# State-space loop: additions and tables moved to GpSimd, coefficients and scan in PSUM, input products in three passes

## The chip, the cores and the metric

The kernel runs on one core of a Trainium2 chip. Five engines of that core work at once, each through its own instructions in a fixed order: TensorE (PE; its weight loads are shown apart as PEld), VectorE (DVE), ScalarE (ACT), GpSimd (POOL) and SyncE (SP), which issues most DMA transfers. A wait at the head of an engine's order holds everything behind it. The metric is the device time of one execution, in microseconds (us). A profiled execution also has a span, from its first instruction to its last.

## The reference

Two residual layers over a sequence of 512 tokens and 1024 channels, all in float32. Layer 0 mixes tokens with a grouped state-space layer (S5), layer 1 with forgetting attention; each is followed by a gated feed-forward part. The change concerns the state-space layer alone:

```python
u = h @ w_in                                  # 512 x 1024, weights 1024 x 1024
lb = exp(lre*dt) * (cos(lim*dt), sin(lim*dt)) # 64 groups of 64 complex states
bb = k * b                                    # complex coefficients, 16 channels a group
state[t] = lb * state[t-1] + bb @ u[t]        # within each group
y[t] = Re(c @ state[t]) + d_skip * u[t]
y = gelu(y); y = y * sigmoid(y @ w_glu); out = y @ w_out
```

Here `h` is the normed input, scaled and shifted by columns that are computed from a conditioning vector.

## The kernel before

Channels lie on the 128 partitions: 8 channel tiles (`KT`) of 128 channels, each with 8 groups, that is 4 pairs of groups. Tokens are cut into 64 blocks of 8 (`L` = 8, `B` = 64). A state is carried from block to block; inside a block a small kernel of matrix products does the work.

The start of the S5 stage is under a manual schedule for PE, ACT, DVE and SP: there these engines take the instructions in the order in which the code is written. GpSimd, and everything behind that part, is put in order by the scheduler. In the start the scale and shift columns are made (`ada_pe`, matrix products over weights that stream in), the scaled input `a_x` is made by 8 DVE instructions, the input product of tile 0 is taken from it without its shift (the shift is added by `u_shift` afterwards), and `s5_params` makes on the DVE, with many small instructions, the powers and coefficients of the states: `s_pr`, `s_pi` (called `er`, `ei` as views), `s_lr`, `s_li`, and `s_mag`. Then the shift is added to `a_x` on the ACT, and `s5_tables` makes the first three doublings of the rotation table `s_rot`.

The loop runs over tiles m = 0 to 7. For each tile:

- `inputs(m)`: 8 products in float32 (weights `raw`, input `a_x`) give the input projection in a PSUM bank of pool `mm`; ACT copies it out (`uf`); it goes through DRAM to the layout `u`.
- `s5_inputs(m)`: `s5_outer` makes the coefficients `x` on the DVE, two multiplications of 1024 elements per partition and an addition. `x` has one buffer, its partner `x2` two. PE multiplies them by `s_cd` (line 993) and transposes them (line 1004); ACT copies `ktt`, `kt` and `w1` out; `kt` goes through DRAM (`s_z`) and comes back as `tw`, from which ACT makes `t`.
- `s5_scan(m)`: PE makes products of `w1` and `u` in a PSUM bank of pool `aux` (line 1026); the DVE turns them with `s_rot`, scans them along the blocks with the factors `cf`, and turns them back to the states `ua`.
- `s5_states_out(m)`: `s5_outer` again, from `er`, `ei` and `cc`, gives `w2`.
- `s5_outputs(m)`: PE products of `t` and `u` (line 1068) and of `w2` and `ua` (line 1076), then the gelu on the ACT.
- every second tile `s5_tables` doubles the table three times for the next 8 pairs (9 instructions).

Both PSUM pools, `mm` and `aux`, have 4 banks. `raw()` takes a weight buffer by its third argument from one of three rings: `raw` (3 buffers), `w_hi` (5) or `w_lo` (5, through `rest`). Elsewhere in the kernel float32 products are made in three passes (`mms`): operand and weight are each split into a part rounded to float32r (hi) and a rest (lo), and hi by hi, hi by lo and lo by hi are summed.

## Time and profile before

| what | value |
|---|---|
| time, median of 3 runs | 1182.35 us (1181.65 to 1184.41) |
| the profiled execution | 1181.21 us |
| its span | 1179.1 us |
| PE clock granted, mean | 0.997 |
| busy: PE, DVE, ACT, POOL | 1161.2, 970.3, 642.4, 99.1 us |

In the rows of a group, "out<-in" gives the tiles by name, then shapes as partitions x elements, then the count, the busy time and the mean of one in ns. A timeline row gives the start, the time from the first start to the last end of the instructions in it, the engine, the line, and in brackets the idle time ahead of it with what ended it. Two instructions of one engine overlap a little: a DVE instruction of 1.22 us starts 1.14 us after one of its kind. A row of the chain gives start, length, engine, tile and line. One float32 matrix product shows as two PE records of 128x512. Line numbers are those of the kernel before; behind the change they are a few higher.

### The profile page before, as it was taken

What the parts mean: (1) busy time and instruction counts of PE and PEld (TensorE: products, weight loads), DVE (VectorE), ACT (ScalarE), POOL (GpSimd) and SP (SyncE); (2) the same over time, 40 slices, a digit from 0 to 9 for tenths busy, and PEclk for the clock granted to TensorE, in tenths of its full rate; (3) what the DMA queues carried; (4) which work ended last, traced back from release to release, by engine and by line L of the source; (5) the groups of instructions that cost most, each with busy time, mean ns of one, the idle gap of its engine ahead of it and who ended that gap; (6) DMA issues with size and microseconds to landing.
All of it is one profiled execution on the core that took longest, in us unless ns stands there. A gap on an engine that the chain in (4) does not pass through costs nothing.

```text
span 1179.1 us, 21197 instructions
## 1 busy us (share of the span) xinstructions
PE 1161.2 (98%) x8199; PEld 1015.6 (86%) x8199; DVE 970.3 (82%) x1805; ACT 642.4 (54%) x1150; POOL 99.1 (8%) x157
## 2 busy tenths in 40 slices
PE   7999999999999999999999999999999999999997
PEld 2466688899999999998998788878999989999987
DVE  8899987889878889876675788866999888888855
ACT  2554536346667667665443657644556545555543
POOL 1000000000011111110000534320000000000000
PEclk9999999999999999999999999999999999999998
DMA  9788868815789899887524555423123323333331
GB/s 356 242 259 256 253 199 308 283 54 145 188 248 255 217 252 253 229 240 209 145 89 151 179 193 187 154 72 109 54 84 114 120 89 104 114 113 108 92 88 72
DMA packets 79427, 202.70 MB, mean 172 GB/s; under 512 B 23919, under 2 KB 26191, under 8 KB 78303
## 3 DMA queue, kind: packets, MB, share of 16 engines
q1 hardware_dynamic: 72847, 181.96, 46.5%
q0 software_dynamic: 6192, 18.88, 9.2%
q8 instruction: 64, 1.05, 0.4%
q10 hardware_dynamic: 288, 0.52, 0.1%
q14 instruction: 36, 0.29, 0.1%
HBM read 194.41 MB, written 6.92 MB: 171 GB/s over the span
## 4 chain that ended last, share of the span: by engine, by line
PE 93%; DMA 3%; DVE 2%; ACT 1%; issue 1%; POOL 0%; SPq 0%; DVEq 0%; ACTq 0%; POOLq 0%
PE mmp L308 43%; PE mmp L568 19%; PE aux L568 7%; PE mmp L1186 4%; PE mmp L1366 3%; PE mmp L1216 2%; PE aux L1512 2%; PE aux L1495 2%; PE aux L1076 1%; PE aux L1068 1%; PE mmp L221 1%; PE aux L1465 1%; DMA raw<-in_ada_w 1%; PE aux L1026 1%; DMA nf<-nfd 1%; PE mmp L1153 1%
## 5 line engine op out<-in xcount | busy, mean ns | idle before, releaser
L287 ACT ACTIVATE w_hi<-raw 128x1024 fp32r<-128x1024 f32 (+4 forms) x197 | 173.4, 888 | 125.8 <-PE mmp L308 64.9
L292 DVE TENSOR_TENSOR w_lo<-raw,w_hi 128x1024 fp32r<-128x1024 f32 (+4 forms) x154 | 155.7, 1013 | 30.2 <-ACT w_hi L287 26.4
L308 PE MATMUL mmp<-ghi,w_hi 128*128 128x512 f32 (+1 forms) x392 | 144.1, 368 | 0.0
L308 PE MATMUL mmp<-glo,w_hi 128*128 128x512 f32 (+1 forms) x392 | 143.7, 367 | 0.0
L308 PE MATMUL mmp<-ghi,w_lo 128*128 128x512 f32 (+1 forms) x392 | 143.6, 366 | 0.0
L308 PE MATMUL mmp<-a_hi,w_hi 128*128 128x256 f32 (+1 forms) x440 | 141.0, 323 | 0.0
L308 PE MATMUL mmp<-a_hi,w_lo 128*128 128x256 f32 (+1 forms) x440 | 139.0, 317 | 0.0
L308 PE MATMUL mmp<-a_lo,w_hi 128*128 128x256 f32 (+1 forms) x440 | 138.8, 316 | 0.0
L568 PE MATMUL mmp<-w_hi 128*128 128x256 f32 x420 | 116.3, 277 | 1.2 <-ACT nm_h L575 1.2
L568 PE MATMUL mmp<-w_lo,w_hi 128*128 128x256 f32 x420 | 116.0, 276 | 0.0
L568 PE MATMUL mmp<-w_hi,w_lo 128*128 128x256 f32 x420 | 116.0, 276 | 0.0
L287 ACT ACTIVATE w_hi<-sums 128x1024 fp32r<-128x1024 f32 x78 | 81.8, 1058 | 43.2 <-DVE sums L539 24.2
L292 DVE TENSOR_TENSOR w_lo<-sums,w_hi 128x1024 fp32r<-128x1024 f32 x78 | 94.3, 1218 | 4.0 <-ACT w_hi L287 2.8
L308 PEld LDWEIGHTS mmp<-a_hi,w_hi 128*128 128x128 f32 x440 | 82.2, 188 | 7.1 <-issue 2.6
L308 PEld LDWEIGHTS mmp<-a_hi,w_lo 128*128 128x128 f32 x440 | 82.6, 188 | 6.4
L308 PEld LDWEIGHTS mmp<-a_lo,w_hi 128*128 128x128 f32 x440 | 82.7, 188 | 4.6
L256 DVE CUSTOM_DVE_ANT_0 ada_raw<-ada_raw,ada_c,rest 128x1024 f32<-128x1024 f32 x64 | 83.7, 1324 | 2.3 <-DMA ada_raw<-in_ada_rows 2.2
L308 PEld LDWEIGHTS mmp<-ghi,w_lo 128*128 128x128 f32 x392 | 73.6, 188 | 12.3
L308 PEld LDWEIGHTS mmp<-glo,w_hi 128*128 128x128 f32 x392 | 73.6, 188 | 11.1
L308 PEld LDWEIGHTS mmp<-ghi,w_hi 128*128 128x128 f32 x392 | 73.6, 188 | 11.1
L568 PEld LDWEIGHTS mmp<-w_hi 128*128 128x128 f32 x420 | 78.8, 188 | 1.8 <-ACT nm_h L575 1.8
L568 PEld LDWEIGHTS mmp<-w_lo,w_hi 128*128 128x128 f32 x420 | 78.9, 188 | 0.0
(331 smaller groups left out, 3047.1 us busy)
## 6 DMA issues: line engine op xcount, KB each, us to landing
raw<-in_w_up SPq DMA_DIRECT2D x88, 512.0 KB, 3.4
ada_raw<-in_ada_rows SPq DMA_DIRECT2D x64, 512.0 KB, 4.6
raw<-in_ada_w SPq DMA_DIRECT2D x32, 512.0 KB, 7.0
...
```

The source lines that it names most:

```text
L221: self.last_mm = nc.tensor.matmul(ps[32 * qq:32 * qq + 32, :], self.sc32[:, k, :], w[:, q * S:(q + 1) * S], start=(step is steps[0]), stop ...
L256: nc.vector.tensor_tensor_reduce(w, w, self.crow, 1.0, self.ada_b[:, i, m:m + 1], ALU.mult, ALU.add, self.par[i][:, m:m + 1])
L287: nc.scalar.activation(hi, src, AF.Copy)
L292: self.late = (nc.vector.tensor_tensor(lo, src, hi.bitcast(F32), ALU.subtract).ins,)
L308: self.last_mm = self.nc.tensor.matmul(o, wt, xt[:, cols], start=(k == 0 and n == 0), stop=(k == nk - 1 and n == 2),)
L568: self.last_mm = nc.tensor.matmul(o, wt[:, k], xt[:, k], start=(first and k == 0 and n == 0), stop=(k == H - 1 and n == 2), skip_group_che ...
L1026: nc.tensor.matmul(ps[g2 * 64:(g2 + 1) * 64, ri, k, :], w1[:, k, ri, g2 * 64:(g2 + 1) * 64], u[:, g2 * H4 + k, :], start=(k == 0 and ri == ...
L1186: nc.tensor.matmul(ps, w[m][:, k, :], x[:, k], start=(k == 0), stop=(k == KT - 1))
L1216: nc.tensor.matmul(gps[m], wt, xt[:, k], start=(k == 0 and part == 0 and xt is yhi), stop=(k == KT - 1 and part == 1))
L1366: self.last_mm = nc.tensor.matmul(ps[q, b][:, :n], xt[:, k, tb], wt, start=(k == 0 and i == 0), stop=(k == KT - 1 and i == 2),)
L1495: nc.tensor.transpose(pt[:, r - rs[0], k, :], s[:, r, k * P:(k + 1) * P], self.ident)
L1512: nc.tensor.matmul(pv[:, c * P:], self.v[:, hp, k, r].rearrange("p t d -> p (t d)"), pp[:, r, c + 3 * k:NB + 3 * k, :].rearrange("p b t -> ...
```

## The change

- `parted(m)` splits the input weights of tiles 1 to 7: ACT makes `w_hi`, GpSimd the rest `w_lo`. `part_x(k)` splits the input: ACT adds the shift and rounds (`a_xhi`, in the room that held `h`), DVE makes the rest (`x_lo`). The input products of tiles 1 to 7 are made by `mms`, three float32r passes each in place of one float32 product.
- the 8 `x_lo` take two buffers of the ring `w_hi` and two of `w_lo` through the loop (`self.rooms` = 3 is the number of `w_lo` buffers left); `load_w` uses the ring `raw` alone, and `ada_pe` the rings `raw` and `w_hi`.
- `in_banks` has ACT copy `lr`, `li` into one PSUM bank of `mm` and `er`, `ei` into another; `s5_outer` reads them there (the output coefficients of tile 7 are still made from SBUF).
- the additions of `s5_outer` go from the DVE to GpSimd, and so do the tables for tiles 2, 4 and 6.
- `s5_scan` works in place: the turned values, the scan and the turning back stay in the PSUM bank of the products, which is free when `ua` is written and no longer after the second multiplication.

```diff
     def s5_outer(self, outs, ls, planes, qs, first):
...
-        return nc.vector.tensor_tensor(outs[0], outs[0], outs[1], ALU.add).ins
+        nc.gpsimd.tensor_tensor(outs[0], outs[0], outs[1], ALU.add)
+        return last.ins
...
-        self.x_made = self.s5_outer((x, x2), (self.lr, self.li), self.bb, qs, (1, 0))
+        self.x_made = self.s5_outer((x, x2), self.lp, self.bb, qs, (1, 0))
...
-        m1 = pool.tile([P, 2, W], F32, name="m1")
         m2 = pool.tile([P, 2, W], F32, name="m2")
-        nc.vector.tensor_tensor(m1, v, cb, ALU.mult)
         nc.vector.tensor_tensor(m2, v, sb, ALU.mult)
-        nc.vector.tensor_tensor(m1[:, 0], m1[:, 0], m2[:, 1], ALU.add)
-        nc.vector.tensor_tensor(m1[:, 1], m1[:, 1], m2[:, 0], ALU.subtract)
+        nc.vector.tensor_tensor(v, v, cb, ALU.mult)
+        nc.vector.tensor_tensor(v[:, 0], v[:, 0], m2[:, 1], ALU.add)
+        nc.vector.tensor_tensor(v[:, 1], v[:, 1], m2[:, 0], ALU.subtract)
...
+        line = ps.rearrange("p r g b -> p (r g b)")
+        nc.vector.tensor_tensor_scan(line, cf.rearrange("p r g b -> p (r g b)"), line, 0.0, op0=ALU.mult, op1=ALU.add)
         a = pool.tile([P, 2, H4, B], F32, name="ua", bufs=2)
+        b = pool.tile([P, 2, W], F32, name="ub")
+        nc.vector.tensor_tensor(b[:, 0], v[:, 0], sb[:, 0], ALU.mult)
+        nc.vector.scalar_tensor_tensor(b[:, 1], v[:, 1], -1.0, sb[:, 1], op0=ALU.mult, op1=ALU.mult)
+        nc.vector.tensor_tensor(v, v, cb, ALU.mult)
+        self.scanned = nc.vector.tensor_tensor(a.rearrange("p r g b -> p r (g b)"), v, b[:, ::-1], ALU.add).ins
...
+                def parted(m):
+                    hi = self.wpool.tile([P, KT, P], F32R, name="w_hi", bufs=WB)
+                    nc.scalar.activation(hi, w[m], AF.Copy)
+                    lo = self.rest([P, KT, P])
+                    nc.gpsimd.tensor_tensor(lo, w[m], hi.bitcast(F32), ALU.subtract)
+                    w[m] = [(hi[:, k], lo[:, k]) for k in range(KT)]
...
+                    def part_x(k):
+                        b = self.par[i][:, k:k + 1]
+                        nc.scalar.activation(xhi[:, k], x[:, k], AF.Identity, bias=b)
+                        return nc.vector.scalar_tensor_tensor(
+                            xlo[k], x[:, k], b, xhi[:, k].bitcast(F32), op0=ALU.add, op1=ALU.subtract
+                        )
...
                     for k in range(2):
-                        nc.scalar.activation(x[:, k], x[:, k], AF.Identity, bias=self.par[i][:, k:k + 1])
+                        part_x(k)
+                    parted(1)
...
                     for k in range(2, KT):
-                        nc.scalar.activation(x[:, k], x[:, k], AF.Identity, bias=self.par[i][:, k:k + 1])
-                    behind = [self.s5_signs_c(), next(params), self.s5_tables(slice(0, G // 2), 0, 3), last_mm.ins]
+                        part_x(k)
+                    behind = [self.s5_signs_c(), next(params), self.s5_tables(slice(0, G // 2), 0, 3, nc.vector), last_mm.ins]
...
                     for k in range(m == 1, KT):
-                        nc.tensor.matmul(ps, w[m][:, k, :], x[:, k], start=(k == 0), stop=(k == KT - 1))
+                        self.mms(ps, w[m], split_x, k, KT, slice(0, S))
...
+            self.lp = in_banks(self.lr, self.li)
             with self.behind(*behind):
                 for m in range(2):
                     inputs(m)
                 ws[0] = self.s5_inputs(0)
+            self.ep = in_banks(self.er, self.ei)
...
-                        self.s5_tables(slice(m * 4, m * 4 + 8), 3, 6)
+                        self.s5_tables(slice(m * 4, m * 4 + 8), 3, 6, nc.gpsimd if m else nc.vector)
```

The first place is the DVE in the start of the stage, behind the 8 instructions that make `a_x`. Before, the small instructions of `s5_params` (`s_pr`, `s_pi`, `s_lr` and so on) stand next:

```order
L174 SCALAR_TENSOR_TENSOR ga_100<-aux,rest 128x8
L1137 SCALAR_TENSOR_TENSOR a_x<-h,ga_100,aux 128x512 x8
L892 TENSOR_TENSOR s_w_360<-s_pr 128x128
L893 TENSOR_TENSOR s_w_361<-s_pi 128x128
L894 TENSOR_TENSOR s_pr<-s_w_360,s_w_361 128x4x32
```

After, on the same engine:

```order
L175 SCALAR_TENSOR_TENSOR ga_100<-aux,rest 128x8
L1141 SCALAR_TENSOR_TENSOR a_x<-h,ga_100,aux 128x512 x8
L1174 SCALAR_TENSOR_TENSOR x_lo<-a_x,par_96,a_xhi 128x512 x8
L893 TENSOR_TENSOR s_w_360<-s_pr 128x128
L894 TENSOR_TENSOR s_w_361<-s_pi 128x128
L895 TENSOR_TENSOR s_pr<-s_w_360,s_w_361 128x4x32
```

The eight `x_lo`, which read the shift columns `par_96` and the `a_xhi` of the ACT, stand ahead of the rest of `s5_params`.

The second place is the ACT, from the copy that writes the shift columns (`par_96`) on. Before:

```order
L177 ACTIVATE par_96<-aux 128x8
L1160 ACTIVATE a_x<-a_x,par_96 128x512 x2
L1170 ACTIVATE u_shift<-aux 128x1
L1172 ACTIVATE uf<-mmp,u_shift 128x512
L241 ACTIVATE c_rows<-aux 8x128
L1175 ACTIVATE a_x<-a_x,par_96 128x512 x6
```

After (the four copies `mmp<-...` are those of `in_banks`; the second `w_hi` is that of tile 2):

```order
L178 ACTIVATE par_96<-aux 128x8
L1173 ACTIVATE a_xhi<-a_x,par_96 128x512 x2
L1107 ACTIVATE w_hi<-raw 128x1024
L1191 ACTIVATE u_shift<-aux 128x1
L1193 ACTIVATE uf<-mmp,u_shift 128x512
L242 ACTIVATE c_rows<-aux 8x128
L1173 ACTIVATE a_xhi<-a_x,par_96 128x512 x6
L822 ACTIVATE s_cc<-s_c 128x32x16
L823 ACTIVATE s_cc<-s_c 128x32x32
L826 ACTIVATE s_cd_133<-s_cc 64x64x16 x2
L1210 ACTIVATE uf<-mmp 128x512
L1245 ACTIVATE mmp<-s_lr 128x256
```

A `w_hi` stands ahead of `u_shift`, and with it ahead of six of the eight `a_xhi`; `w_hi` of tile 2 comes behind the copies of `s_lr` and `s_pr`.

The third place is GpSimd in the loop. Before, it has nothing there, only the memsets of the start and the next stage's first:

```order
L833 MEMSET s_cd_133 128x2048
L837 MEMSET s_mask 128x64
L871 MEMSET s_pr 128x32
L872 MEMSET s_pi 128x32
L838 MEMSET s_mask 128x1
L136 MEMSET z_gap 128x32
```

After, the stretch behind the addition of `x` for tile 2, up to that for tile 3 (`x_974`; `w_926` is `w2` of tile 1):

```order
L945 TENSOR_TENSOR s_tab<-s_rot,s_turn 128x128
L946 TENSOR_TENSOR s_tab<-s_rot,s_turn 128x128
L947 TENSOR_TENSOR s_rot<-s_tab 128x2x8x8
L945 TENSOR_TENSOR s_tab<-s_rot,s_turn 128x256
L946 TENSOR_TENSOR s_tab<-s_rot,s_turn 128x256
L947 TENSOR_TENSOR s_rot<-s_tab 128x2x8x16
L960 TENSOR_TENSOR w_926<-w_926,x_927 128x1024
L945 TENSOR_TENSOR s_tab<-s_rot,s_turn 128x512
L946 TENSOR_TENSOR s_tab<-s_rot,s_turn 128x512
L947 TENSOR_TENSOR s_rot<-s_tab 128x2x8x32
L1109 TENSOR_TENSOR w_lo<-raw,w_hi 128x1024
L960 TENSOR_TENSOR x<-x,x_974 128x1024
```

Nine table instructions, the rest of a weight tile and the addition for `w2` stand between two additions of `x`.

More of the change, by code (lines that the diff above doesn't have):

```diff
@@ L85, in __init__ @@
         self.pending = None
+        self.rooms = WB
         self.rests, self.odd, self.by_dma = 0, False, False
@@ L216, in ada_pe @@
             for j, (t, k) in enumerate(step):
-                w = self.raw([P, D], self.io["ada_w"][i, k * P:(k + 1) * P, t * D:(t + 1) * D], n % 3)
+                w = self.raw([P, D], self.io["ada_w"][i, k * P:(k + 1) * P, t * D:(t + 1) * D], n % (3 if self.rooms == WB else 2))
                 n += 1
@@ L943, in s5_tables @@
             im = self.turn[:, k, 1:3, pairs, None].to_broadcast(sh)
-            nc.vector.tensor_tensor(v1, T[:, :, :, :n], re, ALU.mult)
-            nc.vector.tensor_tensor(v2, T[:, ::-1, :, :n], im, ALU.mult)
-            last = nc.vector.tensor_tensor(T[:, :, :, n:2 * n], v1, v2, ALU.add)
+            e.tensor_tensor(v1, T[:, :, :, :n], re, ALU.mult)
+            e.tensor_tensor(v2, T[:, ::-1, :, :n], im, ALU.mult)
+            last = e.tensor_tensor(T[:, :, :, n:2 * n], v1, v2, ALU.add)
         return last.ins
@@ L954, in s5_outer @@
             a = first[n]
-            nc.vector.tensor_tensor(
+            last = nc.vector.tensor_tensor(
                 o.rearrange("p k r c j -> p k (r c) j"), l[:, qs, None, :].to_broadcast(sh),
@@ L958, in s5_outer @@
             )
-        return nc.vector.tensor_tensor(outs[0], outs[0], outs[1], ALU.add).ins
+        nc.gpsimd.tensor_tensor(outs[0], outs[0], outs[1], ALU.add)
+        return last.ins
     def s5_states_out(self, m):
         t1, t2 = (self.s5q.tile([P, GM // 2, 2, CG, L], F32, name=n, bufs=2) for n in ("w2", "x2"))
-        self.s5_outer((t1, t2), (self.er, self.ei), self.cc, slice(m * (GM // 2), (m + 1) * (GM // 2)), (0, 1))
+        self.s5_outer((t1, t2), (self.er, self.ei) if m == KT - 1 else self.ep, self.cc, slice(m * (GM // 2), (m + 1) * (GM // 2)), (0, 1))
         return t1
@@ L1046, in s5_scan @@
             )
-        sg = m2
-        nc.vector.tensor_tensor_scan(
-            sg.rearrange("p r w -> p (r w)"), cf.rearrange("p r g b -> p (r g b)"),
-            m1.rearrange("p r w -> p (r w)"), 0.0, op0=ALU.mult, op1=ALU.add,
-        )
-        a = pool.tile([P, 2, H4, B], F32, name="ua", bufs=2)
-        b = pool.tile([P, 2, H4, B], F32, name="ub", tag="m1")
-        fl = lambda t: t.rearrange("p r g b -> p r (g b)")
-        nc.vector.tensor_tensor(fl(a), sg, cb, ALU.mult)
-        nc.vector.tensor_tensor(fl(b)[:, 0], sg[:, 0], sb[:, 0], ALU.mult)
-        nc.vector.scalar_tensor_tensor(fl(b)[:, 1], sg[:, 1], -1.0, sb[:, 1], op0=ALU.mult, op1=ALU.mult)
-        self.scanned = nc.vector.tensor_tensor(a, a, b[:, ::-1], ALU.add).ins
+        line = ps.rearrange("p r g b -> p (r g b)")
+        nc.vector.tensor_tensor_scan(line, cf.rearrange("p r g b -> p (r g b)"), line, 0.0, op0=ALU.mult, op1=ALU.add)
+        a = pool.tile([P, 2, H4, B], F32, name="ua", bufs=2)
+        b = pool.tile([P, 2, W], F32, name="ub")
[3 more added lines that the diff above has]
+        self.scanned = nc.vector.tensor_tensor(a.rearrange("p r g b -> p r (g b)"), v, b[:, ::-1], ALU.add).ins
         return a
@@ L1105, in load_w @@
                 def load_w(m):
-                    w[m] = self.raw([P, KT, P], self.io["s5_w_in"][m], m % 3)
+                    w[m] = self.raw([P, KT, P], self.io["s5_w_in"][m])
+                def parted(m):
[4 more added lines that the diff above has]
+                    w[m] = [(hi[:, k], lo[:, k]) for k in range(KT)]
                 self.rot = keep.tile([P, 2, G // 2, B], F32, name="s5_rot")
@@ L1158, in s5 @@
                     )
+                    xhi = self.normed("a_hi", WHOLE, "a_xhi")
+                    self.rooms = WB - 2
+                    xlo = []
+                    for n in range(KT // 2):
+                        tag = ("w_hi", f"w_lo{self.rooms + n // 2}")[n % 2]
+                        xlo.append(self.wpool.tile([P, 2 * S + 32 * (n % 2)], F32R, name="x_lo", tag=tag, bufs=(WB, 1)[n % 2]))
+                    xlo = [t[:, S * k:S * k + S] for t in xlo for k in range(2)]
+                    def part_x(k):
[4 more added lines that the diff above has]
+                        )
+                    split_x = lambda k: (xhi[:, k], xlo[k])
                     for k in range(2):
-                        nc.scalar.activation(x[:, k], x[:, k], AF.Identity, bias=self.par[i][:, k:k + 1])
+                        part_x(k)
+                    parted(1)
                     col = self.aux.tile([P, 1], F32, name="aux")
@@ L1164, in s5 @@
                         if k == KT // 2:
-                            nc.tensor.matmul(second, w[1][:, 0, :], x[:, 0], start=True, stop=False)
+                            self.mms(second, w[1], split_x, 0, KT, slice(0, S))
                         last_mm = nc.tensor.matmul(
@@ L1218, in glu_head, with in_banks @@
                         )
+            def in_banks(*ts):
+                o = self.mm.tile([P, S], F32, name="mmp").rearrange("p (n q j) -> p n q j", n=2, j=L)
+                for n, t in enumerate(ts):
+                    nc.scalar.activation(o[:, n], t, AF.Copy)
+                return o[:, 0], o[:, 1]
+            self.lp = in_banks(self.lr, self.li)
             with self.behind(*behind):
```

6 lines of the change are left out of this document (4 added, 2 removed).

## The prediction

> **What bounds the kernel now.** I read the page first (busy time by engine, then the chain that ended last), then the busy time by stretch, then the chain in order of time through the S5 stage.
>
> ```profile
> PE 1161.2 (98%) x8199; PEld 1015.6 (86%) x8199; DVE 970.3 (82%) x1805; ACT 642.4 (54%) x1150; POOL 99.1 (8%) x157
> PE 93%; DMA 3%; DVE 2%; ACT 1%; issue 1%; POOL 0%; SPq 0%; DVEq 0%; ACTq 0%; POOLq 0%
> 37.00:60.34 23.34, 22.59 (x121) 11.15 (x120) 20.26 (x28) 16.23 (x36) 0.00 (x0) 1.00 0.65 201
> 60.34:135.13 74.79, 74.79 (x660) 46.51 (x656) 71.58 (x105) 36.44 (x104) 0.00 (x0) 1.00 0.82 255
> 135.13:178.40 43.27, 43.27 (x388) 35.64 (x385) 36.47 (x55) 19.43 (x48) 0.46 (x5) 1.00 0.70 222
> ```
>
> The last three rows are the run-up to the loop, five periods of it and its tail, with PE, PEld, DVE, ACT, POOL, granted clock, DMA share and GB/s. TensorE bounds everything: 93% of the chain, and no gap at all in the loop and the tail. VectorE comes close there (71.58 of 74.79), GpSimd does nothing. What the change does to the time is therefore two things: PE work that it removes, and PE idle time that it creates. The chain gives both ends of the loop and the unit prices:
>
> ```profile
> 37.93 0.79 PE aux L1166 x8
> 39.68 0.80 PE aux L1166 x8
> ...
> 53.42 0.57 PE aux L993 x16
> 53.99 1.02 PE aux L1004 x8
> 55.02 0.11 PE aux L970
> ...
> 60.41 1.08 PE aux L1026 x32
> 61.50 1.05 PE mmp L1186 x2
> ...
> 82.25 5.15 PE mmp L1186 x12
> ...
> 135.20 1.08 PE aux L1026 x32
> ...
> 178.40 4.99 PE aux L308 x22
> ```
>
> The scan products (L1026) of tile 0 start at 60.41, those of tile 5 at 135.20: 14.96 us a tile. Six float32 products take 5.15, so 0.858 each; 22 float32r passes take 4.99, so 0.227 each and 0.680 for three.
>
> **The change, part by part: the gain.** Tiles 1 to 7 have 56 products (one is L1165). 56 x (0.858 - 0.680) = 10.0 us of PE work go, all on the path. The loop's work falls by 8 x 0.178 to 13.5 a tile. The additions and tables taken off VectorE (two a tile, and nine a pair of tiles) gain nothing of themselves: the chain has 2% DVE.
>
> **The loss: the start.** Here the order decides. VectorE and ScalarE before:
>
> ```profile
> 24.60 5.36 DVE L1137 SCALAR_TENSOR_TENSOR a_x<-h,ga,aux 128x512 f32<-128x512 f32 x8
> 29.87 0.38 DVE L892 TENSOR_TENSOR s_w<-s_pr 128x128 f32<-128x128 f32 x1
> 33.40 0.63 DVE L894 TENSOR_TENSOR s_lr<-s_w,s_w 128x256 f32<-128x256 f32 x1
> 39.02 1.22 DVE L955 TENSOR_TENSOR x<-s_lr,s_bb 128x1024 f32<-128x1024 f32 x1
> 40.16 1.22 DVE L955 TENSOR_TENSOR x<-s_li,s_bb 128x1024 f32<-128x1024 f32 x1
> 41.30 0.28 DVE L944 TENSOR_TENSOR s_tab<-s_rot,s_turn 128x128 f32<-128x128 f32 x1
> ...
> 37.21 1.33 ACT L1160 ACTIVATE a_x<-a_x,par 128x512 f32<-128x512 f32 x2
> 40.51 0.17 ACT L1170 ACTIVATE u_shift<-aux 128x1 f32<-128x1 f32 x1 [1.96 <-PE aux L1166]
> 41.45 3.77 ACT L1175 ACTIVATE a_x<-a_x,par 128x512 f32<-128x512 f32 x6
> 122.37 1.04 ACT L1240 ACTIVATE w_hi<-raw 128x1024 fp32r<-128x1024 f32 x1
> ```
>
> From 29.87 to 39.02 VectorE does 9.15 us of coefficients and tables while it waits for no shift. After, the eight `x_lo` stand ahead of them, and `x_lo` needs the shift. That cover is gone. GpSimd's prices come from the attention stage, the only rows with its elementwise work:
>
> ```profile
> L1443 POOL TENSOR_TENSOR nf<-nf,rest x16: 1284/1296/2257, 647.4 to 771.9; 128x512 f32<-128x512 f32 x16
> L1486 POOL TENSOR_SCALAR s<-s,sm 128x512 f32<-128x512 f32 x16 | 11.9, 754 | 1.1 <-DVE sm L1484 0.8
> L1486 POOL TENSOR_SCALAR s<-s,sm 128x128 f32<-128x128 f32 x16 | 5.7, 371 | 58.8 <-DVE sm L1484 51.1 <-DVE mn L1477 7.6
> 647.45 3.75 POOL L1443 TENSOR_TENSOR nf<-nf,rest 128x512 f32<-128x512 f32 x2 [21.22 <-DMA nf<-nfd]
> 679.66 2.55 POOL L1443 TENSOR_TENSOR nf<-nf,rest 128x512 f32<-128x512 f32 x2 [3.03 <-DMA nf<-nfd]
> ...
> 648.35 1.71 DVE L256 CUSTOM_DVE_ANT_0 ada_raw<-ada_raw,ada_c,rest 128x1024 f32<-128x1024 f32 x1
> 665.68 1.27 DVE L256 CUSTOM_DVE_ANT_0 ada_raw<-ada_raw,ada_c,rest 128x1024 f32<-128x1024 f32 x1
> 679.70 2.20 DVE L292 TENSOR_TENSOR plo<-aux,phi 128x384 fp32r<-128x384 f32 x4
> ```
>
> No row has 1024 elements. The two `TENSOR_SCALAR` rows give a fixed part of about 0.24 us (754 - 371 over 384 elements, carried back to zero); with it the 1.284 of 512 elements makes 2.04 ns an element, so I take 2.33 for 1024, 0.76 for 256, 0.50 for 128. The ends are VectorE's 1.22 and twice the row, 2.57. [...]
>
> The last rows show that the two engines disturb each other. Beside `plo<-aux,phi`, where VectorE reads one operand in PSUM, a GpSimd pair takes 2.55. Beside L256, which reads SBUF twice, it takes 3.75, 1.2 more, and L256 itself 1.71 for 1.27. So 1.7 us of such VectorE work cost GpSimd 1.2. In the loop nearly all VectorE work now has an operand in PSUM; in the start the table instructions do not.
>
> The walk, each step from the rows above:
>
> 1. `a_xhi` 0 and 1 are ready at 38.54, `w_hi` of tile 1 at 39.6 (+1.04), `w_lo` at 41.9 (+2.33). PE, which reaches the third pass of tile 1's first product before the last four shift columns, ends those (+0.23, +0.80) at 42.9; before at 40.48.
> 2. `u_shift`, `uf` and the six other inputs took from 40.51 to 45.22, 4.7 us: now to 47.6. The last `x_lo` (0.67, as one of the eight of `a_x`, 5.36 / 8) ends at 48.3.
> 3. The 9.15 us of coefficients and tables now run from 48.3 to 57.45. `s_lr` is there 4.2 us into them (33.40 + 0.63 before), so ScalarE's four copies (under 0.67 each, the `a_x` pair of twice their size taking 1.33) and tile 2's `w_hi` are ready inside this time.
> 4. Two multiplications (39.02 to 41.30 before) end at 59.75. The addition on GpSimd: 2.33, plus a disturbance, because eight table instructions start on VectorE at the same moment. By the rows below they have 3 x 0.283 + 3 x 0.418 + 2 x 0.686 = 3.5 us; at 1.2 for 1.7 this is up to 2.5, I take 2.0. `x` of tile 0 is there at 64.1.
> 5. PE: L993 and L1004 (0.57, 1.02), 65.7. `x` has one buffer, so VectorE starts tile 1's only now: 1.14 + 0.6 (a table instruction between) + 1.14, 68.6; addition 2.33, 70.9; L993, L1004, L970 (1.7), 72.6. Only then, in PE's order, come the scan products of tile 0: 72.6 for 60.41, 12.2 us late.
>
> ```profile
> L944 DVE TENSOR_TENSOR s_tab<-s_rot,s_turn 128x512 f32<-128x512 f32 x3 | 2.1, 686 | 0.0
> L944 DVE TENSOR_TENSOR s_tab<-s_rot,s_turn 128x256 f32<-128x256 f32 x3 | 1.3, 418 | 0.0
> L944 DVE TENSOR_TENSOR s_tab<-s_rot,s_turn 128x128 f32<-128x128 f32 x3 | 0.8, 283 | 0.0
> L1037 DVE TENSOR_TENSOR m<-aux,s_rot 128x512 f32<-128x512 f32 x5 | 3.4, 684 | 0.5 <-PE aux L1026 0.5
> L1055 DVE TENSOR_TENSOR ua<-m,s_rot 128x512 f32<-128x512 f32 x5 | 3.4, 682 | 0.0
> ...
> 56.33 0.42 SPq L192 DMA_DIRECT2D raw<-in_s_w_in  x1
> ```
>
> By then PE has done 16 products before, 16 2/3 after, with all else equal; the 2/3 is worth 0.45. PE meanwhile has nothing to do: its order holds only tiles 1 and 2, and tile 2 waits for a `w_hi` that stands behind `s_lr`.
>
> **The loop.** With an operand in PSUM (L1037) VectorE takes 684 ns, without (L1055) 682. [...] ScalarE gets 7 x 1.04 and four small copies; it is half idle. Input weights now come from three `raw` buffers and are held until GpSimd has made the rest; behind such a load `u`, `tw` and `s_z` would wait in SP's order. I take nothing: SP issued tile 3's load at 56.33, 5 us before its first product (61.50), and if that cover goes, a load is late by one GpSimd instruction, 0 to 2.6 us.
>
> GpSimd has, for two tiles, 6 x 2.33 and 3 x (0.50 + 0.76 + 1.28): 21.6 us of 27.0. But between the additions of `x` for tiles 2 and 3 stand twelve instructions: 7.6 + 3 x 2.33 = 14.6, more than PE's 13.5. So PE waits about 1 us for each of tiles 3, 5 and 7. The scan's bank of `aux`, held some 8 us longer, and `t` of tile 0, whose way through DRAM begins late, add a little. I take 3 us in all; the ends are 0 (additions of 1.22) and 17 (2.57, and 1.28 for each table instruction: 19.3, 5.8 too many, three times).
>
> **Sum.** + 12.2 (start) - 0.45 - 39 1/3 x 0.178 = 7.0 (products still to come) + 3 (loop) = +7.7. The tail, from 135 to 178, is continuous PE work before, and that work is unchanged. The profiled execution took 1181.21, 1.1 below the median of 1182.35; on the median's scale +7.7 gives 1190.
>
> **Rivals.**
>
> *GpSimd keeps up* (the other side). If its additions take VectorE's 1.22 and nothing disturbs them, the start is 3 x 1.1 + 2.0 shorter, 6.9 late, and the loop waits for nothing: 6.9 - 0.45 - 7.0 = -0.5, 1182. It turns into a gain where float32r passes also suffer less from being interleaved: a lone float32 product costs 1.05 (row at 61.50) for 0.858; three such places a tile at 0.15 less, over five tiles, make -2.3 more, 1179.5. It decides at additions of about 1.3 us. Against it: no GpSimd row is that fast.
>
> *GpSimd bounds the loop.* Table instructions have broadcast and reversed operands of four dimensions, which no row shows on GpSimd. At 2.57 and 1.28 the pair of tiles has 6 x 2.57 + 9 x 1.28 = 26.9 us, all of PE's 27.0, and the waits go towards the 17: 1195 to 1202. For it: the stretch of twelve instructions. Against it: the first rows of GpSimd, undisturbed, are at 1.284 all.
>
> *PSUM banks.* `aux` has four; two hold outputs, one the scan, and with it held through the turning back, L1004 and L970 share one and wait for ScalarE's copies each time. About 1 us a tile: 1196 to 1199.
>
> **How the numbers follow.** This measurement can tell about 0.2% from no change: 1180.0 to 1184.7 is the same. Forecast (1186 to 1194): 0.50. GpSimd bounds: 0.17. Banks: 0.08. GpSimd keeps up: 0.25, of which 0.12 within the same and 0.13 faster. So faster 0.13, same 0.12, slower 0.75. The range, 1180 to 1200, leaves out the gain and the far end of GpSimd's case; by itself the forecast has 1186 to 1194, from the disturbance (0 to 2.5) and the loop (1 to 6).
>
> **What would show it.** Right: VectorE idle from about 29.9 to 38 and again between the first two and the last six `x_lo`; the first `x` multiplication near 57; PE idle for about 14 us between 37 and 72; scan products of tile 0 near 72; then 13.5 to 14.5 us a tile; three passes of a product near 0.68. Wrong: scan products of tile 0 before 67, or a loop period above 15 (then GpSimd's or the banks' case: `x` late behind L960 and the tables, or L1006 behind copies), or passes that PE cannot run at 0.227 because the weights of each must be loaded anew between other work.

## The result, and the profile after

The changed kernel takes 1201.89 us (median of 4 runs, 1197.25 to 1203.22) against 1182.59 before (now of four runs): ratio 1.0154, 95% interval 1.0124 to 1.0184. It is slower, as forecast, but by 19.3 us and not 7.7, and outside the range of 1180 to 1200. The profiled execution is the fastest of the four, 1197.25 us with a span of 1195.5, 16.4 longer than before; the mean clock of TensorE (PE) is 0.992 in it, 0.985 to 0.986 in the three others, 0.997 before.

The page of the changed kernel: busy times, shares of the chain, and the two stretches shown of the kernel before (columns as there):

```profile
PE 1162.0 (97%) x8255; PEld 1031.0 (86%) x8255; DVE 955.3 (80%) x1770; ACT 650.6 (54%) x1161; POOL 173.8 (15%) x207
PE 85%; DVE 6%; DMA 5%; ACT 1%; issue 1%; POOL 1%; SPq 0%; DVEq 0%; POOLq 0%; ACTq 0%
37.00:60.34 23.34, 15.47 (x53) 11.22 (x53) 15.05 (x29) 15.19 (x28) 4.71 (x2) 0.76 0.44 149
60.34:135.13 74.79, 68.97 (x645) 51.18 (x644) 55.76 (x72) 37.44 (x99) 53.34 (x37) 0.96 0.72 227
```

PE has 10 us less to do by the sum and is busy for as long as before, 1162.0 for 1161.2. The column behind POOL says most of why: the granted clock, 1.00 before in both stretches, is 0.76 and 0.96, and work at a lower clock takes longer: the eight shift columns at 42.99 in the chain below take 1.51 us, and 0.80 before. In windows of 2 us it is seen where (same columns):

```profile
40.00:42.00 2.00, 0.49 (x2) 0.06 (x1) 0.00 (x0) 0.00 (x0) 2.00 (x1) 1.00 0.00 0
42.00:44.00 2.00, 1.80 (x8) 1.71 (x8) 0.00 (x0) 0.00 (x0) 0.15 (x1) 0.53 0.42 74
46.00:48.00 2.00, 2.00 (x6) 1.26 (x5) 1.79 (x3) 2.00 (x5) 0.00 (x0) 0.50 0.51 166
50.00:52.00 2.00, 2.00 (x10) 1.36 (x8) 1.93 (x6) 1.90 (x3) 0.00 (x0) 1.00 0.94 291
54.00:56.00 2.00, 0.00 (x0) 0.00 (x0) 1.93 (x4) 1.55 (x3) 0.00 (x0) 0.94 0.53 201
60.00:62.00 2.00, 2.00 (x6) 1.56 (x5) 1.90 (x6) 0.20 (x1) 0.00 (x0) 0.50 0.94 269
```

PE stands idle for most of 40 to 42 and for all of 54 to 56, and behind each gap it works at half clock (0.50), though in 46 to 48 and in 60 to 62 it is busy without a break. The stretches at clock 0.50 begin at 42.1 (6.83 us long), 55.8 (6.83) and 76.2 (3.41). The PE timeline of the same kernel (start, length, instruction, idle ahead of it):

```profile
42.20 0.79 PE L309 MATMUL mmp<-a_xhi,w_lo 128*128 128x512 f32 x1 [1.71 <-POOL w_lo L1109]
44.95 0.63 PE L309 MATMUL mmp<-x_lo,w_hi 128*128 128x512 f32 x1
45.38 0.63 PE L309 MATMUL mmp<-a_xhi,w_lo 128*128 128x512 f32 x1
...
50.08 0.39 PE L309 MATMUL mmp<-x_lo,w_hi 128*128 128x512 f32 x1
50.31 0.39 PE L309 MATMUL mmp<-a_xhi,w_lo 128*128 128x512 f32 x1
...
56.17 0.79 PE L309 MATMUL mmp<-a_xhi,w_hi 128*128 128x512 f32 x1 [4.12 <-ACT w_hi L1107]
58.61 0.79 PE L309 MATMUL mmp<-a_xhi,w_lo 128*128 128x512 f32 x1 [1.21 <-POOL w_lo L1109]
66.33 0.64 PE L995 MATMUL aux<-x,s_cd 128*32 128x128 f32 x16 [2.16 <-POOL x L960]
74.84 0.65 PE L995 MATMUL aux<-x,s_cd 128*32 128x128 f32 x16 [2.38 <-POOL x L960]
```

The same pass starts 0.43 us behind the one ahead at 45, and 0.23 at 50. The chain in order of time shows what the start waits for:

```profile
42.20 0.79 PE mmp L309
42.99 1.51 PE aux L1187 x8
44.53 0.18 ACT u_shift L1191
...
50.28 0.32 DVE s_w L893
...
56.30 2.31 DVE s_ring L722
...
61.59 2.27 DVE x L956 x2
...
64.05 2.38 DVE s_tab L946
...
69.40 1.14 DVE x L956
...
72.44 2.35 POOL x L960
74.84 0.65 PE aux L995 x16
...
76.85 1.91 PE aux L1028 x32
```

The scan products of tile 0 (L1028) start at 76.85, for a forecast of 72.6 and 60.41 before, and take 1.91 us for 1.08. Between 44.5 and 74.8 PE is not in the chain: from 46.2 to 74.5 VectorE works without a pause of more than 0.11 us, and what PE does meanwhile ends ahead of its waits for `x` (2.16 and 2.38 us). By this chain a slow pass in that time costs nothing of itself; only the work at half clock ahead of 44.5 and behind 74.8 does.

The account of PE up to the chain's row of 22 passes, which starts at 192.90 for 178.40 before (+14.5): I summed for each kind of work the time from the start of each group in the PE timeline to the start of the next, less the idle shown.

| | before | after | difference |
|---|---|---|---|
| idle | 0.8 | 14.4 | +13.6 |
| input products, tile 0's ahead of the plus sign | 58.0 | 7.6 + 48.4 (168 passes) | -2.0 |
| scan products, shift columns, `ada` groups, rest | | | +2.9 |

The sum is +14.5. It says what PE did with the time, not what held it up: of the 48.4, work at half clock that stands ahead of a wait would have been idle instead. Behind this row another 1.9 us are lost, 1.4 of them between 388 and 560 us; the trace names no cause.

### The profile page after: what moved, and what is told of

It reads as the page before. It is cut to its first block, busy times and chain, and to the rows that moved or that the text cites. A ratio compares the mean times of both kernels' runs of the same rounds, so it can differ in the third digit from the quotient of the medians.

```text
span 1195.5 us, 21380 instructions
## 1 busy us (share of the span) xinstructions
PE 1162.0 (97%) x8255; PEld 1031.0 (86%) x8255; DVE 955.3 (80%) x1770; ACT 650.6 (54%) x1161; POOL 173.8 (15%) x207
## 3 DMA queue, kind: packets, MB, share of 16 engines
q8 instruction: 65, 1.06, 0.4%
## 4 chain that ended last, share of the span: by engine, by line
PE 85%; DVE 6%; DMA 5%; ACT 1%; issue 1%; POOL 1%; SPq 0%; DVEq 0%; POOLq 0%; ACTq 0%
PE mmp L309 44%; PE mmp L569 18%; PE aux L569 7%; PE mmp L1397 3%; DMA raw<-in_w_up 2%; PE aux L1543 2%; PE mmp L1238 2%; PE aux L1526 1%; PE aux L1073 1%; PE aux L1496 1%; PE aux L1065 1%; DMA yt<-s_yd 1%; PE mmp L1125 1%; PE aux L1028 1%; DMA nf<-nfd 1%
## 5 line engine op out<-in xcount | busy, mean ns | idle before, releaser
L309 PE MATMUL mmp<-ghi,w_hi 128*128 128x512 f32 (+1 forms) x392 | 144.1, 368 | 0.0
L309 PE MATMUL mmp<-glo,w_hi 128*128 128x512 f32 (+1 forms) x392 | 143.7, 367 | 0.0
L309 PE MATMUL mmp<-ghi,w_lo 128*128 128x512 f32 (+1 forms) x392 | 143.6, 366 | 0.0
L309 PE MATMUL mmp<-a_hi,w_hi 128*128 128x256 f32 (+1 forms) x440 | 141.0, 323 | 0.0
L309 PE MATMUL mmp<-a_hi,w_lo 128*128 128x256 f32 (+1 forms) x440 | 139.0, 317 | 0.0
L309 PE MATMUL mmp<-a_lo,w_hi 128*128 128x256 f32 (+1 forms) x440 | 138.8, 316 | 0.0
L309 PEld LDWEIGHTS mmp<-a_hi,w_hi 128*128 128x128 f32 x440 | 82.2, 188 | 7.1 <-issue 2.6
L309 PEld LDWEIGHTS mmp<-a_hi,w_lo 128*128 128x128 f32 x440 | 82.6, 188 | 6.4
L309 PEld LDWEIGHTS mmp<-a_lo,w_hi 128*128 128x128 f32 x440 | 82.8, 188 | 4.6
L309 PEld LDWEIGHTS mmp<-ghi,w_lo 128*128 128x128 f32 x392 | 73.6, 188 | 12.3
L309 PEld LDWEIGHTS mmp<-glo,w_hi 128*128 128x128 f32 x392 | 73.6, 188 | 11.2
L309 PEld LDWEIGHTS mmp<-ghi,w_hi 128*128 128x128 f32 x392 | 73.6, 188 | 11.1
L540 DVE TENSOR_TENSOR sums<-raw 128x512 f32<-128x512 f32 x70 | 46.1, 688 | 42.3 <-DMA raw<-in_w_up 42.3
```

Of the source, the lines that this page charges most:

```text
L309: self.last_mm = self.nc.tensor.matmul(o, wt, xt[:, cols], start=(k == 0 and n == 0), stop=(k == nk - 1 and n == 2),)
L540: sub = lambda o, u, v, op=ALU.subtract: nc.vector.tensor_tensor(o, u, v, op)
```

## The experiments

### Each half alone

*adds_alone*: the changed kernel with its input products in float32, as before. `parted` and `part_x` go; additions, tables and PSUM operands stay.

```diff
-                        self.mms(ps, w[m], split_x, k, KT, slice(0, S))
+                        nc.tensor.matmul(ps, w[m][:, k, :], x[:, k], start=(k == 0), stop=(k == KT - 1))
```

> Additions and tables on GpSimd, coefficients and scan in PSUM; input products in float32 as in the kernel before. Theory (the loss comes from the three passes' order of the start): x of tile 0 is wanted by PE only near 53 us and the addition ends near 44 to 46, so nothing is late; the loop stays PE's at 14.96 us a tile: 1180 to 1185. Rival (GpSimd bounds the loop or the two engines' disturbance makes the loss): 1190 or more, with a period above 15.2 us.

Measured: 1188.16, ratio 1.0033 (1.0020 to 1.0047), 3 us above what was expected and below the rival's 1190. In the stretch of five loop periods:

```profile
60.34:135.13 74.79, 74.79 (x663) 46.26 (x653) 50.46 (x66) 38.03 (x107) 42.55 (x38) 1.00 0.80 258
```

VectorE is relieved (50.46 for 71.58), GpSimd is at 57%, PE has no gap, the clock is 1.00. There are two waits elsewhere, 0.99 us for GpSimd's `x` of tile 1 and 1.40 for `a_hi` in the tail. GpSimd does not bound the loop of this kernel; this half costs some 4 us, and not 19.

*passes_alone*: three passes with rests by GpSimd; additions, tables and scan as before.

```diff
-        nc.gpsimd.tensor_tensor(outs[0], outs[0], outs[1], ALU.add)
-        return last.ins
+        return nc.vector.tensor_tensor(outs[0], outs[0], outs[1], ALU.add).ins
```

> Three passes with the weights' rests on GpSimd; additions and tables on VectorE, coefficients and scan in SBUF as in the kernel before. Theory: the start is late as in the changed kernel less the addition's place (scan products of tile 0 at 70 to 75 us for 76.85), the passes after idle are slow as there, and the loop is VectorE's, at its 14.3 us a tile and not 13.5: 1193 to 1203. Rival (GpSimd's additions make the loss): 1174 to 1182.

Measured: 1212.09, ratio 1.0233 (1.0208 to 1.0258), 9 us above the theory's range. Windows of 25 us:

```profile
125.00:150.00 25.00, 23.99 (x244) 17.54 (x242) 24.90 (x36) 12.46 (x33) 2.64 (x1) 1.00 0.74 230
150.00:175.00 25.00, 18.19 (x187) 16.02 (x187) 20.88 (x31) 13.83 (x36) 0.00 (x0) 0.73 0.39 118
```

VectorE is full in the first window (24.90 of 25), and PE spends 30.7 us at half clock. The loss comes with the passes; beside them the move to GpSimd saves some 9 us (1.0154 for 1.0233).

### What idle costs

*coeff_first* puts the coefficients and tables ahead of the first `x_lo`:

```diff
+                    ready = [next(params), self.s5_tables(slice(0, G // 2), 0, 3, nc.vector)]
                     for k in range(2):
                         part_x(k)
...
-                    behind = [self.s5_signs_c(), next(params), self.s5_tables(slice(0, G // 2), 0, 3, nc.vector), last_mm.ins]
+                    behind = [self.s5_signs_c(), *ready, last_mm.ins]
```

> Only the order of the start changes: VectorE does the coefficients and the first tables (9.15 us) ahead of x_lo 0 and 1, as in the kernel before, and the multiplications for tile 0 come between x_lo 1 and 2. Theory (order of the start makes PE idle, and the idle makes the granted clock fall): PE idle between 37 and 77 us falls from about 13 to under 4 us, its passes there stand 0.23 us apart and not 0.43, and the time goes to 1177 to 1185. Rival 1 (the idle costs only itself, the slow passes have another cause): 1187 to 1192, passes still at 0.43 in the stretch 44 to 49. Rival 2 (GpSimd's additions bound the loop, the start is cover): 1198 to 1203, unchanged within 4 us.

Measured: 1199.77, ratio 1.0135 (1.0117 to 1.0153). Idle up to 216 us fell from 14.4 to 10.5 only, and the stretches at half clock grew from 17.1 to 23.9 us. PE timeline, then windows behind the gap:

```profile
81.22 0.50 PE L309 MATMUL mmp<-a_xhi,w_lo 128*128 128x512 f32 x1 [3.28 <-POOL w_lo L1109]
```

```profile
78.00:80.00 2.00, 0.00 (x0) 0.00 (x0) 0.66 (x1) 2.00 (x7) 2.00 (x2) 1.00 0.85 246
90.00:92.00 2.00, 2.00 (x6) 1.57 (x5) 2.00 (x3) 1.95 (x7) 0.55 (x1) 0.50 0.98 275
```

A start that is earlier runs into `w_lo` of tile 3, which stands behind tables on GpSimd. The gap of 3.28 us is followed by 10.24 us at half clock, 82.7 to 92.9, with PE busy in all of it: 5.1 us more. The scan products of tile 0 start at 70.4, 6 us earlier than in the changed kernel, and the time stays the same. So the order of the start was not the whole cause; my theory fell in that. The time is the second rival's (1198 to 1203), and at this place, the `w_lo` of tile 3, so is the mechanism.

*fill_idle* gives the changed kernel 33 passes without use where PE waits:

```diff
                         if k == KT // 2:
+                            for _ in range(10):
+                                nc.tensor.matmul(second, w[1][0][0], xhi[:, 0], start=True, stop=True, skip_group_check=True)
                             self.mms(second, w[1], split_x, 0, KT, slice(0, S))
...
+                    if m == 2:
+                        with tc.issue_after(self.last_mm.ins):
+                            for _ in range(23):
+                                nc.tensor.matmul(ps, w[1][0][0], xhi[:, 0], start=True, stop=True, skip_group_check=True)
```

> The changed kernel with 33 extra passes (128x512 fp32r, 0.227 us each at full clock) on PE where it stands idle: ten ahead of tile 1's first product, 23 ahead of tile 2's. They go into the bank that the first real pass clears, so nothing else is computed. They add 7.5 us of PE work and no result. Theory (idle lowers the granted clock afterwards): passes between 42 and 64 us stand 0.23 us apart and not 0.43, the clock of that stretch is 1.00 and not 0.86, and in spite of the extra work the time falls by 3 to 8 us, to 1194 to 1199. Rival (the slow passes are slow for themselves, by their weights or by fp32r): passes stay at 0.43, and the time is 1202 to 1210.

Measured: 1199.86, ratio 1.0138 (1.0123 to 1.0153), above the theory's 1194 to 1199. The PE timeline:

```profile
39.10 2.58 PE L1187 MATMUL mmp<-a_xhi,w_hi 128*128 128x512 f32 x10 [0.83 <-ACT w_hi L1107]
...
46.24 0.40 PE L309 MATMUL mmp<-a_xhi,w_hi 128*128 128x512 f32 x1
46.47 0.39 PE L309 MATMUL mmp<-x_lo,w_hi 128*128 128x512 f32 x1
...
65.11 1.08 PE L995 MATMUL aux<-x,s_cd 128*32 128x128 f32 x16 [6.06 <-POOL x L960]
```

The passes of tile 1 stand at 0.23: they are not slow for themselves. But the filler does not make `x` earlier; the idle moved to one gap of 6.06 us, with half clock behind it (6.83 us from 62.1). The chain says what the full clock was worth:

```profile
42.36 0.80 PE aux L1189 x8
...
75.46 1.85 PE mmp L222 x14
77.31 1.08 PE aux L1028 x32
```

The shift columns (L1189 here) end at 43.16, 1.3 us earlier than in the changed kernel, and PE is through with the products of tile 1's `x` at 75.46, 1.4 us earlier. The passes between, at full clock now, brought nothing more. With 7.5 us of added work the time stayed the same within the intervals.

*gap_alone* and *gap_filled* test the price of idle in the kernel before, without any part of the change:

```diff
-                    for k in range(m == 1, KT):
-                        nc.tensor.matmul(ps, w[m][:, k, :], x[:, k], start=(k == 0), stop=(k == KT - 1))
+                    ks = list(range(KT)) if m != 1 else [7] + [k for k in range(1, KT) if k != 7]
+                    for k in ks:
+                        nc.tensor.matmul(ps, w[m][:, k, :], x[:, k], start=(m != 1 and k == 0), stop=(k == ks[-1]))
```

and for *gap_filled* besides:

```diff
+                    late = self.aux.tile([P, S], F32, name="aux")
+                    for _ in range(4):
+                        nc.tensor.matmul(late, w[0][:, 0, :], x[:, 0], start=True, stop=True)
```

> The kernel before, float32 products and all, with one edit: tile 1's products of k 1 to 7 begin with k = 7, whose input ScalarE shifts last (near 45.2 us). PE, with 0.8 us of idle there before, stands about 2 us ahead of the transposes of x and 1.3 ahead of the product: +2.6 us of idle, nothing else. Theory (idle of a third of a 3.41 us stretch brings stretches at half clock): at least one stretch of 3.41 us at clock 0.50 behind it, as PE works on all of it 1.7 us each, one to three of them: +4.3 to +7.7, 1187 to 1191. Rival (idle costs only itself): +2.6 or less, 1184.5 to 1186, clock 1.00 throughout.

> gap_alone with four extra float32 products (128x512, 0.858 us each) on PE behind the shift's columns, into a bank that nothing reads: PE does 3.43 us of useless work where it stood idle. Theory: no stretch at half clock; +3.4 of work less the idle that it covers: +2.5 to +3.2 against the kernel before, 1185 to 1187, and not slower than gap_alone although it does more. Rival: the same or up to 1 us slower than gap_alone.

Measured, 12 runs each: 1187.88 for gap_alone, ratio 1.0030 (1.0017 to 1.0044), inside the theory's range; 1184.93 for gap_filled, ratio 1.0007 (0.9997 to 1.0018), just below it. gap_alone, PE timeline and windows:

```profile
42.67 1.94 PE L1004 MATMUL aux<-rest,x 128*128 128x128 f32 x8 [2.49 <-DVE x L959]
```

```profile
40.00:42.00 2.00, 0.18 (x2) 0.00 (x0) 2.00 (x4) 1.97 (x5) 0.00 (x0) 0.81 0.01 2
44.00:46.00 2.00, 2.00 (x5) 1.08 (x4) 1.97 (x4) 2.00 (x3) 0.00 (x0) 0.50 0.90 338
```

gap_filled, the same:

```profile
39.62 3.68 PE L1171 MATMUL aux<-a_x,raw 128*128 128x512 f32 x8
43.47 1.04 PE L1004 MATMUL aux<-rest,x 128*128 128x128 f32 x8
```

```profile
44.00:46.00 2.00, 2.00 (x9) 1.11 (x8) 1.97 (x4) 2.00 (x4) 0.00 (x0) 1.00 0.42 82
```

One gap of 2.49 us brings 6.83 us at half clock, 5.41 of them with PE at work: the eight L1004 take 1.94 for 1.04. With 3.43 us more work in place of the gap PE stays at 1.00 and the kernel is 2.95 us faster in the medians; the two intervals overlap by 0.0001, and eight of the twelve runs of gap_alone are slower than the slowest of gap_filled. So the half clock comes from the idle, and here, where PE is the engine that all else waits for, filling it pays even with useless work. One run of gap_alone took 1183.41 us at a mean clock of 0.998 (the others 0.995 to 0.997; 0.997 to 0.999 in the kernel before): the gap may not lower the clock every time, but no trace of that run shows it.

### Mending the order

*tables_later*, on top of coeff_first:

```diff
-                    if m % 2 == 0:
-                        self.s5_tables(slice(m * 4, m * 4 + 8), 3, 6, nc.gpsimd if m else nc.vector)
+                    if m == 0:
+                        self.s5_tables(slice(0, 8), 3, 6, nc.vector)
...
+                    if m % 2 and m < KT - 1:
+                        with tc.issue_after(self.rest_made):
+                            self.s5_tables(slice(m * 4 + 4, m * 4 + 12), 3, 6, nc.gpsimd)
```

> coeff_first (coefficients ahead of x_lo), and on GpSimd the tables of a pair of tiles are made one tile earlier and behind the weights' rest of the next tile, so that w_lo of tile 3 no longer stands behind twelve other instructions. Theory (each stretch of 3.41 us in which PE is idle for a third or more is followed by whole stretches of 3.41 us at clock 0.50): the gap of 3.28 us at 78 us and the 10.24 us at half clock behind it go, the start's gaps and half clock stay: 1199.8 - 3.3 - 5.1 = 1191, 1188 to 1195. Rival (the time is lost elsewhere in the loop, to GpSimd in general): 1197 to 1202.

Measured: 1194.61, ratio 1.0098 (1.0080 to 1.0116), inside the theory's range. The gap at 78 and the half clock behind it are gone; idle is 8.3 us. The start still has 17.1 us at half clock. Here the PE account shows one more cost. The float32 products of the next layer's columns (L222), in groups of 8 before, are cut by the planner:

```profile
112.31 1.06 PE L222 MATMUL mmp<-raw,sc 128*32 128x512 f32 x8
126.00 1.05 PE L222 MATMUL mmp<-raw,sc 128*32 128x512 f32 x2
```

Two records cost what eight cost. From 24 to 200 us the same 96 records stand in 18 groups for 12 and take 19.3 us for 13.5.

*start_mended*: tile 1 in float32 again, `x` shifted in place and split for tile 2 behind it.

```diff
-                            self.mms(second, w[1], split_x, 0, KT, slice(0, S))
+                            nc.tensor.matmul(second, w[1][:, 0, :], x[:, 0], start=True, stop=False)
...
                     for k in range(2, KT):
+                        add_x(k)
+                    load_w(2)
+                    parted(2)
+                    for k in range(KT):
                         part_x(k)
```

> The changed kernel with another start: coefficients first, tile 1's products in float32 as in the kernel before (they need no rest of the weights), x_hi and x_lo made from the shifted x behind it, ahead of the signs of c. Loop and GpSimd order are the planner's. Theory: PE is busy from 38 to 60 us without a stretch at half clock; what is left is a gap at tile 3, where w_lo stands behind the tables (up to 3.3 us and up to 5 us of half clock): 1178 to 1188. Rival (start is not the cause): 1196 to 1203.

Measured: 1200.75, ratio 1.0154 (1.0137 to 1.0170): a miss, and the rival's time (1196 to 1203). PE waits 3.16 us for an `x_lo` at 49 and some 2 us each for `x` at 62 and 117, for `w_lo` at 89 and for `a_hi` at 180.

*start_and_tables* joins the two.

```diff
+                    if m % 2 and m < KT - 1:
+                        with tc.issue_after(self.rest_made):
+                            self.s5_tables(slice(m * 4 + 4, m * 4 + 12), 3, 6, nc.gpsimd)
```

> Both mended: the start of start_mended and the table order of tables_later. Theory: under 4 us of PE idle up to 200 us and no stretch at half clock, so the gain of the passes comes through, less 8 x 0.178 = 1.4 for tile 1: 1182.5 - 8.6 + 1 to 4 = 1175 to 1178, up to 1181 if one stretch at half clock stays. Rival (passes cost PE more than 0.227 in the loop even at full clock): 1182 to 1188.

Measured: 1197.12, ratio 1.0124 (1.0100 to 1.0148): a miss, above the rival's 1182 to 1188 too. Idle is 11.9 us, half clock 13.7 us. VectorE and GpSimd in this kernel:

```profile
43.41 2.48 DVE L946 TENSOR_TENSOR s_tab<-s_rot,s_turn 128x128 f32<-128x128 f32 x1
47.58 2.68 DVE L945 TENSOR_TENSOR s_tab<-s_rot,s_turn 128x512 f32<-128x512 f32 x1
```

```profile
43.38 2.36 POOL L960 TENSOR_TENSOR x<-x,x 128x1024 f32<-128x1024 f32 x1 [39.62 <-DVE x L956]
47.14 2.57 POOL L1109 TENSOR_TENSOR w_lo<-raw,w_hi 128x1024 fp32r<-128x1024 f32 x1 [1.39 <-ACT w_hi L1107]
```

Table instructions of 0.28 and 0.69 us take 2.48 and 2.68: each ends behind the GpSimd instruction that runs beside it, by 0.15 and 0.55 us. The `x_lo` behind these tables start at 51.50, and PE waits 3.16 us for the first.

*rest2_on_vector* takes that GpSimd instruction out of the way.

```diff
-                    parted(2)
+                    parted(2, nc.vector)
...
-                        self.s5_tables(slice(0, 8), 3, 6, nc.vector)
+                        with tc.issue_after(self.x_parted):
+                            self.s5_tables(slice(0, 8), 3, 6, nc.vector)
```

> start_and_tables, but the weights' rest of tile 2 is made on VectorE and VectorE's tables k 3 to 5 of tiles 0 and 1 come behind the eight x_lo, so that no GpSimd instruction runs beside VectorE's work on two SBUF operands before PE needs x_lo. Theory (GpSimd and VectorE exclude each other there: L945 took 2.68 us beside w_lo for 0.69, and x_lo came 3.16 us late): the gap of 3.16 us at 49 and the stretch at half clock behind it go, passes of tile 2 start near 49: 1197.1 - 3 - 1.5 = 1192 to 1194. Rival (x_lo is late for its own length): gap stays above 2 us, 1196 to 1199.

Measured: 1200.11, ratio 1.0130 (1.0101 to 1.0159): a miss. The gap at 49 is gone, as said, and with GpSimd at rest beside them the two table instructions take 0.28 and 0.69 again; but the time did not fall. The wait for `x` of tile 1 is 3.22 us for 2.05, and two later gaps, 1.82 us for `ua` at 109 and 1.31 for `w_hi` at 157, were each followed by 10.24 us at half clock.

*signs_on_vector* moves the signs of c too.

```diff
-        nc.scalar.activation(self.cc[:, :, 0], c[:, :, 0], AF.Copy)
+        nc.vector.tensor_copy(self.cc[:, :, 0], c[:, :, 0])
```

> rest2_on_vector, and the signs of c (four copies, 3.8 us on ScalarE) move to VectorE ahead of the multiplications for tile 0, so that the L995 group of tile 0 runs before tile 2's passes and x of tile 1 is no longer waited for (gap of 2.05 us at 62.7 in start_and_tables, and the stretch at half clock behind it). Theory: idle of PE up to 200 us under 6 us, at most one stretch at half clock; the passes of tiles 2 to 7 save what they measured at full clock (43.3 us of float32 products become about 36 to 37): 1183 - 6.5 + 5 - 0.8 = about 1181, 1178 to 1186. Rival (the three-pass loop costs more than these gaps and the clock explain): 1188 or more.

Measured: 1201.56, ratio 1.0148 (1.0131 to 1.0165). From 38 to 57 us PE has but one gap over 0.2 us, of 0.70; between 58 and 179 it has ten over 0.25 us, behind `x` (3.30), `w1` (3.54), `kt` (1.60), `t` (1.10), `a_hi` (3.24), on three engines. The time is the rival's (1188 or more), but not for its reason: gaps over 0.2 us add up to 16.8 for the 6 expected, and the stretches at half clock to 17.1. The loop in this order does not keep PE fed.

*fill_mended* is tables_later with filler:

```diff
+                            for _ in range(3):
+                                nc.tensor.matmul(second, w[0][:, 0, :], x[:, 0], start=True, stop=True, skip_group_check=True)
                             self.mms(second, w[1], split_x, 0, KT, slice(0, S))
```

> tables_later with three extra float32 products (2.57 us) on PE behind the first four shift columns, where it waits 0.83 us for w_hi and 1.42 us for w_lo of tile 1; they go into the bank that the first real pass clears. Order of all else in the start as in tables_later. Theory: the 13.65 us at half clock from 39.1 go (PE was busy in 10.8 of them, so 5.4 us), the extra work lies in the waits: 1194.6 - 5 = 1189 to 1190, range 1187 to 1192. Rival (passes are slow for themselves): 1194 to 1196.

Measured: 1196.26, ratio 1.0110 (1.0091 to 1.0130): a miss. The half clock from 39 is gone, as said. Behind gaps of 0.67, 0.64 and 1.45 us between 52 and 56 there is a new stretch of 6.83, and one of 3.41 at 178; that the filler's own 2.57 us ate the rest is not shown.

## Why the prediction was right and wrong

The sum had four terms. Here they are, with what it left out, beside the two profiled executions, cut at the start of the scan products of tile 0 and at the chain's row of 22 passes:

| term | forecast | measured |
|---|---|---|
| scan products of tile 0 late | +12.2 | +16.4 |
| input products (with the 2/3 done before) | -0.45 - 7.0 | -5.3 |
| idle behind the start | +3 | +1.8 |
| other PE work behind the start | 0 | +1.6 |
| behind the row of 22 passes | 0 | +1.9 |
| sum | +7.7 | +16.4 |

**The step that failed is the start, "+ 12.2"**: it was 16.4, by steps 1 to 5 of the walk.

- Steps 1 and 2: `w_lo` came at 42.1 for 41.9. But PE, behind its idle, did the first pass and the shift columns at half clock, which the walk did not have: 0.79 and 1.51 us for 0.23 and 0.80. They end at 44.5 for 42.9, and the last `x_lo` ends at 50.3 for 48.3.
- Step 3: 9.15 us of coefficients and tables became 11.3, and step 4's disturbance of 2.0 us on GpSimd was nil. In the rows below where VectorE reads SBUF twice, one of the two engines stands until the other has ended, and the walk had the wrong one wait. VectorE and GpSimd of the changed kernel:

```profile
56.30 2.30 DVE L722 TENSOR_TENSOR s_ring<-s_ring 128x32 f32<-128x32 f32 x1
63.97 2.45 DVE L946 TENSOR_TENSOR s_tab<-s_rot,s_turn 128x128 f32<-128x128 f32 x1
```

```profile
56.20 2.35 POOL L1109 TENSOR_TENSOR w_lo<-raw,w_hi 128x1024 fp32r<-128x1024 f32 x1 [14.05 <-ACT w_hi L1107]
63.93 2.34 POOL L960 TENSOR_TENSOR x<-x,x 128x1024 f32<-128x1024 f32 x1 [5.38 <-DVE x L956]
```

  GpSimd, which starts first, goes on at its 2.35, and VectorE, with both operands in SBUF, waits until it has ended: 2.30 us for the 0.19 that the one of its kind ahead of it takes, 2.45 for 0.28. A multiplication with an operand in PSUM keeps its 1.22 beside the same addition (at 73.32). In the prediction's row at 647.45 the second instruction of GpSimd's pair starts at 648.94, behind L256 (648.35), and there it is GpSimd that waits, 2.26 us for 1.284. In all of these rows the engine that started first went on.
- Steps 4 and 5: the first `x` multiplication starts at 61.5 for 57.45. That of tile 1 starts at 69.40 for 65.7, since the tables ahead of it were held up once more. L1006 and L972 at half clock add 0.2 us, and the scan products start at 76.85 for 72.6.

**The gain**, "56 x (0.858 - 0.680) = 10.0 us", was mis-sized too. In PE's busy time it came out at 2.0. The 168 passes were to take 0.227 each, 38.1, and took 48.4. 23 of them ran at half clock, 11.2 for 5.2 us; 21 of these lie ahead of 63 us, in front of the waits for `x`, where being faster would have made longer waits. 22 stand first in a run of passes, at 0.322, and 23 last, at 0.291: +3.6. The 100 between are at 0.234: +0.7. The products removed had taken 2.3 more than 56 x 0.858. I took 0.227 from a row of 22 passes in line, at a clock of 1.00. The prediction's own list of what would make it wrong had "passes that PE cannot run at 0.227"; it had the cause only in part, since nothing in the text lets idle lower the clock. It was there to be asked: the page gives the granted clock by stretch, and the forecast itself made 14 us of idle.

**The idle** was forecast at about 14 us between 37 and 72 us, and 3 in the loop. The gaps of the PE timeline add up to 12.4 us from 38 to 75, and to 2.0 elsewhere. That was right in kind, place and size. The size is in part luck: at full clock the same waits would have been longer.

**GpSimd's price** was right: 2.35 for 2.33; the table instructions are cheaper, 0.41, 0.62 and 1.06 for 0.50, 0.76 and 1.28. The waits for `x` of tiles 3, 5 and 7 did not come: behind 76.85 PE has no gap of over 0.2 us for GpSimd. The loop's period is (148.79 - 76.85) / 5 = 14.4 us, within "13.5 to 14.5", but for other reasons: passes in short runs, and a wait of 1.28 us at 99.6. That one is the load that I priced at nothing (0 to 2.6). In the SP queue of the changed kernel

```profile
93.35 0.33 SPq L193 DMA_DIRECT2D raw<-in_s_w_in  x1
```

a weight load waits until GpSimd frees a `raw` buffer (`w_lo`, 90.96 to 93.33), `tw` behind it lands late, and `ktt` on ScalarE behind that.

**The rivals.** GpSimd bounds the loop: no, its time of 1195 to 1202 was met, its mechanism not: the loop's one wait that goes back to GpSimd is the 1.28 us above. In coeff_first, with an earlier start, it does hold the loop, 3.28 us at tile 3. PSUM banks: no wait for one was seen. GpSimd keeps up: the loop kept up, the start did not.

**Where each part stood.** The direction, the place and the order of the waits were right, and the sizes of the start and of the gain were not. PE did 15.3 us of its work at half clock, 7.7 us longer than at full clock, but most of that lay in front of waits. By the chain some 1.5 us of it are in the start's 16.4 and about as much behind it (an estimate from the rows of L309, L1187, L1006, L972 and L1028). The three other runs are 4 to 6 us slower still, at a mean clock 0.0065 lower; no trace of them shows where, and so the part of the median's 19.3 us beyond the profiled 16.4 is open. Whether a fixed order of the loop could keep 13.5 us a tile is open too; no order tried was faster than the kernel before, and the best, tables_later, is 1% slower.
